# Handing a PEER kernel a second, transposed copy of its expert table

## The chip, the cores and the metric

The kernel runs on one core of one Trainium2 chip. The metric is the device time of one execution in microseconds (us). Three runs of the kernel before took 2838.91, 2841.39 and 2841.68 us; the median is 2841.39 us.

## The reference, cut to what matters

The reference is a decoder block over 1024 tokens of 1024 features (and 16 meta tokens ahead of them): a mixer of short convolutions, and behind it a layer of 16384 single-neuron experts. Only the second part is touched. For each token a router picks 8 x 16 experts by product keys (`e1 * 128 + e2`) with a gate for each; `u` and `v` are tables of 16384 rows of 1024.

```python
idx = e1 * PEER_N_KEYS + e2
gates = jax.nn.softmax(vals.astype(jnp.float32), axis=-1).astype(q.dtype)
...
u_sel = jnp.take(u, idx, axis=0)
act = jax.nn.gelu(jnp.einsum("chkd,cd->chk", u_sel, xc))
v_sel = jnp.take(v, idx, axis=0)
return jnp.einsum("chk,chkd->cd", act * gates, v_sel)
```

The result is added to the stream `h`, and a last RMS norm with the gain `final_norm_g` gives the output.

## The kernel before, in words

Tokens go in eight tiles of 128. The five tiles `ND` take the experts densely: every token against all 16384 experts, in 128 chunks of 128 experts (`NK` chunks), weighted with a gate matrix that is zero where the router chose nothing. The three tiles `NG` gather: for each token its 128 rows of `u` and then of `v` are fetched from DRAM, one indirect DMA of 128 rows at a time (L590, issued by POOL), and each fetched block is worked off by one VectorE instruction (L613 for `u`, L639 for `v`). Both ways run side by side.

There are three stages. `front` (mixer, router scores, up to about 700 us) is not touched but for where its constants lie. `gate_matrix` (L656, some 700 to 990 us) builds the gate matrix with TensorE products of one-hot tiles (L693 to L710) and writes it to DRAM; between its steps it lets the generator `hidden_ahead` (L762) run, which computes the `u` products of the 16 chunks in `AHEAD` and parks their gelu in DRAM. `dense` (L784, 990 us to the end) runs over the 128 chunks.

All matrix products are of three passes in 32-bit: each operand is split into a rounded part `hi` (a ScalarE copy, L156) and a rest `lo` (a subtraction, L157, on VectorE or on the engine given), and `mm3` (L183 to L190) multiplies hi by hi, hi by lo and lo by hi.

One chunk of `dense` that is not in `AHEAD` goes so. The chunk of `u` lies in DRAM as 128 experts x 1024 features, but the product needs features on the partitions. So `prep_u` (L729) loads it to `raw` (one pool tag of three buffers, which the chunks of `v` use too), transposes four 128x128 blocks on TensorE into a PSUM bank of the pool `ptr` (L735), and splits that bank to `uhi` and `ulo`; twice a chunk, `q` = 0 and 1, for the chunk that comes next. The product of all 640 dense tokens is made in two segments of 320 columns, each in a PSUM bank `mm` of the pool `pmm` (two banks). The order is q outside, segment inside: q0 of both segments, then q1 of both; each `hidden` call is 12 matmuls of 320 columns (four blocks, three passes), so 48 a chunk. When a segment is complete, ScalarE makes the gelu (L842), VectorE weighs it with the gates (L825), and it is split to `phi` and `plo`. Then the chunk of `v` is loaded and split to `vhi` and `vlo`. After each four chunks `down` (L801) makes the second product: 5 token tiles x 2 halves, each 12 matmuls of 512 columns into a bank `ms` (pool `pms`, four banks), added to `acc` by VectorE (L809).

Between these steps `advance(n)` moves the stream of the gather on by n blocks: three a chunk, one for an `AHEAD` chunk, and `PACE` says how many behind each piece of `down`. A block is fetched (eight buffers `g` in the pool `gb`) and used six blocks later. When a token tile is done, `finish` (L648) makes the last norm with `gfin`, a 128-fold copy of `final_norm_g` that is loaded once, and stores the rows. The dense tiles are finished one after the other in the last `down`.

`hidden_ahead` has its own preparation, `prep_ahead` (L740): four transposes (L747), a ScalarE copy to `uhi` (L751), one more TensorE product that subtracts `uhi` in the bank by way of the constant `minus` (L752), and a second ScalarE copy to `ulo` (L753). Its products go to banks of `pms`.

The order of each engine's instructions is laid down when the program is built, by a planner that follows the order of the code and its priorities; each engine, and each DMA queue, then takes its instructions in that order. The loads of `u`, `v` and the gates all go by SyncE's queue (SP).

## Time and profile before

| | before |
|---|---|
| median of three runs | 2841.39 us |
| the profiled execution's own time | 2840.61 us |
| its span in the profile | 2838.8 us |
| TensorE matmul (PE) busy, share of the span | 2700.6 us, 95% |
| VectorE (DVE) busy | 2443.3 us, 86% |
| ScalarE (ACT) busy | 897.6 us, 32% |
| GpSimd (POOL) busy | 913.7 us, 32% |
| bytes moved by DMA | 684.08 MB |
| of them the gather's indirect DMAs | 402.70 MB |

How to read it: busy time is a sum over the whole span, and the stages differ. Matmuls are pipelined, so one of them lasts longer in the profile than the time until the next one starts; where the text counts what a matmul costs, it takes the distance of starts. The page has 40 slices of equal length with the busy tenths of each engine; windows give the same for stretches that one chooses; groups of instructions carry the mean length of one and the idle time of the engine just before them.

### The profile page before, as it was taken

The page shows a single profiled execution, that of the slowest core. Times are in us where ns is not written, and L with a number is a line of the kernel's source. Part 1 is how long each engine was busy: PE and PEld are TensorE (multiplying, and loading weights), DVE is VectorE, ACT ScalarE, POOL GpSimd, SP SyncE. Part 2 cuts the span into 40 slices and gives each one's busy share as a digit, 9 for nine tenths or more (in the row PEclk, how much of TensorE's full clock was granted, in tenths as well). Part 3 has the DMA queues.
Part 4 walks back from the last instruction along what each step waited for, and adds up shares of the span by engine and source line. Part 5 has one row for each costly group of instructions (what it writes and reads, how often), then busy time and mean ns, then how long its engine had stood idle before and what let it go on. Part 6 is the DMA issues. An engine that isn't in the chain of part 4 may idle for free.

```text
span 2838.8 us, 43868 instructions
## 1 busy us (share of the span) xinstructions
PE 2700.6 (95%) x16513; PEld 2483.4 (87%) x16513; DVE 2443.3 (86%) x5152; ACT 897.6 (32%) x1764; POOL 913.7 (32%) x793
## 2 busy tenths in 40 slices
PE   6999999998999889999999999999999999999998
PEld 5999889987999878988888889888888888888887
DVE  5998667997988778899889889889998888989986
ACT  4112531115998622222222222222222222222222
POOL 0000011110000034455444544445545544545440
PEclk9999999998999999999999999999999999999999
DMA  3111321102576798999989999989999999989992
GB/s 114 45 45 61 103 104 39 38 16 79 156 199 196 229 343 310 335 324 327 331 307 333 313 326 336 331 304 355 329 332 315 331 328 322 324 300 331 327 326 77
DMA packets 299540, 684.08 MB, mean 241 GB/s; under 512 B 20617, under 2 KB 153737, under 8 KB 299328
## 3 DMA queue, kind: packets, MB, share of 16 engines
q0 software_dynamic: 110592, 402.70, 39.7%
q1 hardware_dynamic: 188256, 276.92, 29.2%
q8 instruction: 130, 2.13, 0.3%
q10 hardware_dynamic: 480, 1.65, 0.2%
q14 instruction: 82, 0.67, 0.1%
HBM read 624.05 MB, written 57.15 MB: 240 GB/s over the span
## 4 chain that ended last, share of the span: by engine, by line
PE 67%; DVE 16%; DMA 10%; ACT 4%; issue 2%; SPq 0%; DVEq 0%; ACTq 0%
PE ms L190 12%; PE ms L189 12%; PE ms L188 12%; DMA raw<-in_peer_v_dram 8%; PE mm L190 7%; PE mm L188 7%; PE mm L189 7%; PE mm L707 4%; DVE row L639 3%; DVE vlo L157 2%; PE tr L735 2%; DVE g L613 1%; DMA raw<-in_peer_u_dram 1%; DVE s L469 1%; ACT vhi L156 1%
## 5 line engine op out<-in xcount | busy, mean ns | idle before, releaser
L590 POOL DMA_INDIRECT g<-in_peer_u_dram,ix x384 | 433.5, 1129 | 801.1 <-DVE g L613 374.6
L188 PE MATMUL mm<-nhi,uhi 128*128 128x320 f32 x1792 | 572.4, 319 | 30.2 <-ACT p L842 30.1
L590 POOL DMA_INDIRECT g<-in_peer_v_dram,ix x384 | 438.2, 1141 | 457.2 <-DVE row L639 388.7
L190 PE MATMUL mm<-nhi,ulo 128*128 128x320 f32 x1792 | 557.7, 312 | 17.8 <-DVE ulo L157 17.0
L189 PE MATMUL mm<-nlo,uhi 128*128 128x320 f32 x1792 | 554.1, 309 | 0.0
L188 PE MATMUL ms<-vhi,phi 128*128 128x512 f32 x1280 | 501.1, 391 | 1.5 <-ACT phi L156 1.5
L190 PE MATMUL ms<-vhi,plo 128*128 128x512 f32 x1280 | 498.4, 390 | 0.0
L189 PE MATMUL ms<-vlo,phi 128*128 128x512 f32 x1280 | 498.4, 389 | 0.0
L639 DVE SCALAR_TENSOR_TENSOR row<-g,w,row 128x1024 f32<-128x1024 f32 x384 | 492.1, 1281 | 6.8 <-DMA row<-hd 5.5
L613 DVE SCALAR_TENSOR_TENSOR g<-g,row 128x1024 f32<-128x1024 f32 x384 | 464.5, 1222 | 0.0
L188 PEld LDWEIGHTS mm<-nhi,uhi 128*128 128x128 f32 x1792 | 337.9, 189 | 40.1 <-ACT p L842 38.4
L190 PEld LDWEIGHTS mm<-nhi,ulo 128*128 128x128 f32 x1792 | 337.1, 188 | 28.2 <-DVE ulo L157 28.0
L189 PEld LDWEIGHTS mm<-nlo,uhi 128*128 128x128 f32 x1792 | 338.2, 189 | 1.2
L156 ACT CAST phi<-p 128x320 fp32r<-128x320 f32 x256 | 116.3, 459 | 563.5 <-PE ms L189 340.9
L188 PEld LDWEIGHTS ms<-vhi,phi 128*128 128x128 f32 x1280 | 240.3, 188 | 51.0 <-ACT phi L156 2.4
L190 PEld LDWEIGHTS ms<-vhi,plo 128*128 128x128 f32 x1280 | 240.3, 188 | 50.7 <-DVE plo L157 0.5
L189 PEld LDWEIGHTS ms<-vlo,phi 128*128 128x128 f32 x1280 | 240.4, 188 | 49.1
L156 ACT CAST vhi<-raw 128x1024 fp32r<-128x1024 f32 x128 | 132.9, 1050 | 461.1 <-PE ms L190 316.2
L809 DVE TENSOR_TENSOR acc<-acc,ms 128x512 f32<-128x512 f32 x320 | 219.3, 685 | 34.8 <-PE ms L190 34.0
L157 POOL TENSOR_TENSOR wlo<-wraw,whi 128x1024 fp32r<-128x1024 f32 x16 | 38.0, 2377 | 570.5 <-ACT whi L156 570.5
L157 DVE TENSOR_TENSOR vlo<-raw,vhi 128x1024 fp32r<-128x1024 f32 x128 | 156.3, 1221 | 64.9 <-ACT vhi L156 64.8
L157 DVE TENSOR_TENSOR ulo<-tr,uhi 128x512 fp32r<-128x512 f32 x224 | 153.5, 687 | 43.5 <-ACT uhi L156 42.9
(208 smaller groups left out, 4943.6 us busy)
## 6 DMA issues: line engine op xcount, KB each, us to landing
raw<-in_peer_u_dram SPq DMA_DIRECT2D x128, 512.0 KB, 6.3
raw<-in_peer_v_dram SPq DMA_DIRECT2D x128, 512.0 KB, 6.5
gd<-st SPq DMA_DIRECT2D x40, 1024.0 KB, 9.1
g<-gd SPq DMA_DIRECT2D x64, 640.0 KB, 7.4
wraw<-in_w_in_dram SPq DMA_DIRECT2D x20, 512.0 KB, 4.3
wraw<-in_peer_w_q_dram SPq DMA_DIRECT2D x16, 512.0 KB, 4.1
g<-in_peer_u_dram,ix POOLq DMA_INDIRECT x384, 6.2
g<-in_peer_v_dram,ix POOLq DMA_INDIRECT x384, 6.2
```

The lines of the kernel that those rows point to most:

```text
L156: nc.scalar.copy(hi, src)
L157: self.mark(eng.tensor_tensor(lo, src, hi.bitcast(F32), op=OP.subtract))
L188: self.nc.tensor.matmul(ps, lh(a), rh(b), start=first and i == 0, stop=False)
L189: self.nc.tensor.matmul(ps, lh(a), rl(b), start=False, stop=False)
L190: last = self.nc.tensor.matmul(ps, ll(a), rh(b), start=False, stop=final and i == n - 1)
L469: nc.vector.match_replace(s2, v[:, 0:8], s, NEG)
L590: self.nc.gpsimd.indirect_dma_start(out=g, out_offset=None, in_=self.t[table][0], in_offset=bass.IndirectOffsetOnAxis(ap=ix, axis=0))
L613: self.after(nc.vector.scalar_tensor_tensor(ut, ut, 1.0, b["x"], op0=OP.mult, op1=OP.mult, accum_out=b["act"][:, k:k + 1]))
L639: self.after(nc.vector.scalar_tensor_tensor(b["h"], b.pop(k), res[0][:, k:k + 1], b["h"], op0=OP.mult, op1=OP.add))
L707: nc.tensor.matmul(pg[:, :, m], o2[:, 4 * z + m, :], o1[:, 4 * z + m, :], start=True, stop=True)
L735: self.nc.tensor.transpose(ps[:, k, :], self.raw[:, (4 * q + k) * P:(4 * q + k + 1) * P], self.ident)
L809: self.mark(V.tensor_tensor(acc[:, i, dd], acc[:, i, dd], po, op=OP.add))
```

## The change

`kernel()` makes a second layout of `u` on the host and hands it over as an input `peer_ut`: for each chunk 128 rows (features within a block) by 1024 (8 blocks of 128 experts), so that a chunk lands in SBUF as the product needs it. The gather reads `peer_u` as before.

- `prep_u` and `prep_ahead` go, with their transposes and the constant `minus`. `load_u` loads a chunk of `peer_ut` into a tag `uraw` of two buffers, and `split_u` splits it whole, 128x1024, from SBUF. `uhi` and `ulo` are 128x1024 with two buffers (before 128x512 with three). In `hidden_ahead` the rest `ulo` is made by GpSimd.
- `load_v` has the tag `raw` for itself, with two buffers.
- The order of a chunk's product is now segment outside, q inside. In `dense` the first segment has its bank in `pmm` and the second in `ptr`, so each has two; in `hidden_ahead` both are in `ptr`, two banks in place of the four of `pms`.
- A chunk's `u` is loaded two chunks ahead and split one chunk ahead, behind the first 12 of the 48 matmuls of the chunk before it.
- `advance` is called as often as before: three times a chunk.
- `gfin` goes. `finish` loads `final_norm_g` each time, by SyncE's queue into one of the eight buffers `g` of the gather.
- The constants are given up before the gather's pools are opened; `nT` is allocated ahead of them.

The diff, without the removed `load`, `prep_u` and `prep_ahead`:

```diff
@@ -64,7 +64,6 @@
         self.ctx, self.tc, self.nc, self.t = ctx, tc, tc.nc, t
         self.n = 0
         self.last = {}
-        self.const = ctx.enter_context(self.pool("const", 1))
         self.small = ctx.enter_context(self.pool("small", 2))
         self.keep = ctx.enter_context(self.pool("keep", 1))
         self.ptr = ctx.enter_context(self.pool("ptr", 2, space=PSUM))
@@ -94,8 +93,6 @@
         make_identity(nc, self.ident)
         self.identb = self.tile(const, [P, P], BF16, "identb")
         nc.scalar.copy(self.identb, self.ident)
-        self.minus = self.tile(const, [P, P], F32R, "minus")
-        nc.scalar.mul(self.minus, self.ident, -1.0)
         self.ones = self.tile(const, [P, P], F32, "ones")
         nc.vector.memset(self.ones, 1.0 / C)
         nrow = SCW + CFW + 5
@@ -581,10 +578,6 @@
             yield from self.gather_up(r, w)
             yield from self.gather_down(r, w)
 
-    def gather_constants(self):
-        self.gfin = self.tile(self.ga, [P, D], F32, "gfin", bufs=1)
-        self.nc.scalar.dma_start(self.gfin, self.t["final_norm_g"].rearrange("(o d) -> o d", o=1).broadcast_to([P, D]))
-
     def fetch(self, table, ix):
         g = self.tile(self.gb, [P, D], F32, "g")
         self.nc.gpsimd.indirect_dma_start(out=g, out_offset=None, in_=self.t[table][0],
@@ -647,7 +640,9 @@
 
     def finish(self, ti, h):
         o = self.tile(self.ga, [P, D], F32, "row")
-        self.row_norms([(o, h, P)], self.gfin, None)
+        g = self.tile(self.gb, [P, D], F32, "g")
+        self.nc.sync.dma_start(g, self.t["final_norm_g"].rearrange("(o d) -> o d", o=1).broadcast_to([P, D]))
+        self.row_norms([(o, h, P)], g, None)
         self.nc.sync.dma_start(self.t["out"][0, ti * P:(ti + 1) * P], o)
 
     def key_bank(self):
@@ -721,64 +716,50 @@
             for _ in ahead:
                 pass
 
...
+    def load_u(self, c):
+
+        r = self.tile(self.de, [P, D], F32, "uraw", bufs=2)
+        self.nc.sync.dma_start(r, self.t["peer_ut"][c * P:(c + 1) * P])
         return r
 
...
+    def load_v(self, c):
+        r = self.tile(self.de, [P, D], F32, "raw", bufs=2)
+        self.nc.sync.dma_start(r, self.t["peer_v"][0, c * NK:(c + 1) * NK])
+        return r
+
+    def split_u(self, raw, eng=None):
+        hi, lo = (self.tile(self.de, [P, D], F32R, "u" + s, bufs=2) for s in ("hi", "lo"))
+        self.split(hi, lo, raw, eng=eng)
         return hi, lo
 
     def hidden(self, ps, uT, q, s):
 
         (hi, lo), (xh, xl) = uT, self.nT
-        self.mm3(ps, (lambda a: hi[:, a, :], lambda a: lo[:, a, :]), (lambda b: xh[:, b, s], lambda b: xl[:, b, s]),
-                 [(k, 4 * q + k) for k in range(4)], q == 0, q == 1)
+        at = lambda u: lambda k: u[:, k * NK:(k + 1) * NK]
+        self.mm3(ps, (at(hi), at(lo)), (lambda k: xh[:, k, s], lambda k: xl[:, k, s]),
+                 [(k, k) for k in range(4 * q, 4 * q + 4)], q == 0, q == 1)
 
     def hidden_ahead(self, pool):
 
         T = ND * P
         segs = segments(T)
-        uT = self.prep_ahead(AHEAD[0], 0)
+        raws = [self.load_u(c) for c in AHEAD[:2]]
+        uT = self.split_u(raws.pop(0), eng=self.nc.gpsimd)
         for i, c in enumerate(AHEAD):
-            pu = [self.tile(self.pms, [P, 512], F32, "ms")[:, :s.stop - s.start] for s in segs]
-            for q in range(2):
-                cur = uT
-                for s, ps in zip(segs, pu):
+            pu = [self.tile(self.ptr, [P, 512], F32, "tr")[:, :s.stop - s.start] for s in segs]
+            cur = uT
+            for j, (s, ps) in enumerate(zip(segs, pu)):
+                for q in range(2):
                     self.hidden(ps, cur, q, s)
                     if q == 1:
                         p = self.tile(pool, [P, segs[0].stop], F32, "pa")[:, :s.stop - s.start]
                         self.nc.scalar.activation(p, ps, AF.Gelu_apprx_tanh)
                         self.nc.sync.dma_start(self.p_d[i, :, s], p)
-                    if s is segs[0]:
-                        if q == 0:
-                            uT = self.prep_ahead(c, 1)
-                        elif i + 1 < len(AHEAD):
-                            uT = self.prep_ahead(AHEAD[i + 1], 0)
+                    if j == 0 and q == 0:
+                        if raws:
+                            uT = self.split_u(raws.pop(0), eng=self.nc.gpsimd)
+                        if i + 2 < len(AHEAD):
+                            raws.append(self.load_u(AHEAD[i + 2]))
                     yield
 
     def dense(self, stream):
@@ -812,7 +793,8 @@
                         self.finish(i, acc[:, i, :])
 
             main = [c for c in range(NK) if c not in AHEAD]
-            uT = [self.prep_u(main[0], q) for q in range(2)]
+            raws = [self.load_u(c) for c in main[:2]]
+            nxt = self.split_u(raws.pop(0))
             for c in range(NK):
                 if c % 2 == 0:
                     gg = self.tile(de, [P, T // GB_T, 2, GB_T], F32, "g")
@@ -833,24 +815,28 @@
                     advance(AHD)
                 else:
                     main.pop(0)
-                    pu = [self.tile(self.pmm, [P, 512], F32, "mm")[:, :s.stop - s.start] for s in segs]
-                    for q in range(2):
-                        for s, ps in zip(segs, pu):
-                            self.hidden(ps, uT[q], q, s)
+                    uT = nxt
+                    for j, s in enumerate(segs):
+                        ps = self.tile(*((self.pmm, [P, 512], F32, "mm"), (self.ptr, [P, 512], F32, "tr"))[j % 2])
+                        ps = ps[:, :s.stop - s.start]
+                        for q in range(2):
+                            self.hidden(ps, uT, q, s)
                             if q == 1:
                                 p = self.tile(dn, [P, segs[0].stop], F32, "p")[:, :s.stop - s.start]
                                 nc.scalar.activation(p, ps, AF.Gelu_apprx_tanh)
                                 weigh(s, p)
+                            if j or q:
                                 advance(1)
-                        if main:
-                            uT[q] = self.prep_u(main[0], q)
-                        if q == 0:
-                            advance(1)
+                            if j == 0 and q == 0:
+                                if main:
+                                    nxt = self.split_u(raws.pop(0))
+                                if len(main) > 1:
+                                    raws.append(self.load_u(main[1]))
                 if len(pend) == GRP:
                     down()
                     pend = []
                 vh, vl = (self.tile(dn, [P, D], F32R, "v" + s, bufs=GRP) for s in ("hi", "lo"))
-                self.split(vh, vl, self.load("peer_v", c))
+                self.split(vh, vl, self.load_v(c))
                 pend.append((ph, pl, vh, vl))
             for _ in stream:
                 pass
@@ -860,8 +846,10 @@
 def body(tc, t):
     with ExitStack() as ctx:
         b = Block(ctx, tc, t)
+        b.nT = b.pair(ctx.enter_context(b.pool("nT", 1)), ND * P, "n")
+        const_ctx = b.pool("const", 1)
+        b.const = const_ctx.__enter__()
         b.constants()
-        b.nT = b.pair(ctx.enter_context(b.pool("nT", 1)), ND * P, "n")
         route_ctx = b.pool("route", 2)
         with b.pool("wst", 2, right=True) as b.wst:
             first, routes = b.front(route_ctx)
@@ -869,9 +857,9 @@
         b.gate_matrix(first, routes[:ND - 1])
         gather = [b.token_experts(r) for r in routes[ND - 1:]]
         route_ctx.__exit__(None, None, None)
+        const_ctx.__exit__(None, None, None)
         b.ga = ctx.enter_context(b.pool("ga", 2))
         b.gb = ctx.enter_context(b.pool("gb", GB))
-        b.gather_constants()
         b.last = {}
         b.dense(b.stream(gather))
 
@@ -888,6 +876,9 @@
         a = np.ascontiguousarray(inputs[name])
         arrays[f"in_{name}_dram"] = a
         t[name] = nc.dram_tensor(f"in_{name}_dram", a.shape, mybir.dt.from_np(a.dtype), kind="ExternalInput").ap()
+    ut = np.ascontiguousarray(inputs["peer_u"][0].reshape(NK, NK, KD, P).transpose(0, 3, 2, 1).reshape(NK * P, D))
+    arrays["in_peer_ut_dram"] = ut
+    t["peer_ut"] = nc.dram_tensor("in_peer_ut_dram", ut.shape, F32, kind="ExternalInput").ap()
     t["out"] = nc.dram_tensor("out_0_dram", (1, SEQ, D), F32, kind="ExternalOutput").ap()
     with tile.TileContext(nc) as tc:
         body(tc, t)
```

25 lines of the change are left out of this document (removed).

## The prediction

> **What bounds the kernel now.** I read the page's busy shares and slices first, to see where the stages lie.
>
> ```profile
> span 2838.8 us, 43868 instructions
> ...
> PE   6999999998999889999999999999999999999998
> ...
> DVE  5998667997988778899889889889998888989986
> ...
> GB/s 114 45 45 61 103 104 39 38 16 79 156 199 196 229 343 310 335 324 327 331 307 333 313 326 336 331 304 355 329 332 315 331 328 322 324 300 331 327 326 77
> ```
>
> A slice is 71 us. TensorE (PE) is at nine tenths in nearly all of them, VectorE (DVE) at eight or nine, and from the fifteenth slice on, where the dense stage begins, the DMA moves 300 to 355 GB/s. The change works in the gate stage (some 700 to 990 us) and the dense stage, so I asked for windows of these and of the tail.
>
> ```profile
> core 0: us, PE busy (x) PEld busy (x) DVE busy (x) ACT busy (x) POOL busy (x), PEclk, DMA share, GB/s
> 700.00:990.00 290.00, 277.54 (x2220) 263.89 (x2219) 251.68 (x587) 243.82 (x595) 2.08 (x2) 0.99 0.66 188
> 990.00:2790.00 1800.00, 1738.93 (x9864) 1569.45 (x9863) 1592.78 (x2334) 449.01 (x833) 869.62 (x767) 1.00 0.91 323
> ```
>
> In the dense window, 1800 us long, PE is busy 1739 us, VectorE 1593 us, and the DMA engines 0.91 of the time. That is the difficulty of this case: PE is the bound, but two others stand close behind it. Next I took the groups of the dense window, each with its mean and with the idle time just before it.
>
> ```profile
> L188 PE MATMUL mm<-nhi,uhi 128*128 128x320 f32 x1757 | 561.2, 320 | 30.2 <-ACT p L842 30.1
> L190 PE MATMUL mm<-nhi,ulo 128*128 128x320 f32 x1758 | 547.2, 312 | 17.8 <-DVE ulo L157 17.0
> L639 DVE SCALAR_TENSOR_TENSOR row<-g,w,row 128x1024 f32<-128x1024 f32 x384 | 492.1, 1281 | 6.8 <-DMA row<-hd 5.5
> L188 PE MATMUL ms<-vhi,phi 128*128 128x512 f32 x1240 | 485.5, 392 | 1.5 <-ACT phi L156 1.5
> L809 DVE TENSOR_TENSOR acc<-acc,ms 128x512 f32<-128x512 f32 x310 | 212.5, 685 | 30.5 <-PE ms L190 29.7
> L157 DVE TENSOR_TENSOR vlo<-raw,vhi 128x1024 fp32r<-128x1024 f32 x125 | 152.6, 1221 | 58.5 <-ACT vhi L156 58.5
> L157 DVE TENSOR_TENSOR ulo<-tr,uhi 128x512 fp32r<-128x512 f32 x219 | 150.1, 687 | 43.5 <-ACT uhi L156 42.9
> L735 PE MATMUL tr<-ident,raw 128*128 128x128 f32 x872 | 131.7, 274 | 11.6 <-DMA raw<-in_peer_u_dram 11.5
> L156 ACT CAST vhi<-raw 128x1024 fp32r<-128x1024 f32 x125 | 129.8, 1050 | 450.7 <-PE ms L190 316.2 <-DMA raw<-in_peer_v_dram 134.5
> L156 ACT CAST uhi<-tr 128x512 fp32r<-128x512 f32 x219 | 128.0, 584 | 189.1 <-PE tr L735 185.7 <-PE mm L189 3.3
> L157 DVE TENSOR_TENSOR plo<-p,phi 128x320 fp32r<-128x320 f32 x252 | 123.4, 490 | 35.1 <-ACT phi L156 34.6
> L825 DVE TENSOR_TENSOR p<-p,g 128x320 f32<-128x320 f32 x252 | 121.8, 489 | 31.1 <-ACT p L842 30.9
> ```
>
> A matmul's own length says too much, since the next one starts before it ends. Two pieces of the timeline give the distances: the start of a row is its first column.
>
> ```profile
> 1604.65 0.31 PE L190 MATMUL mm<-nhi,ulo 128*128 128x320 f32 x1
> ...
> 1604.80 0.60 PE L735 MATMUL tr<-ident,raw 128*128 128x128 f32 x4
> ...
> 1605.15 0.39 PE L188 MATMUL mm<-nhi,uhi 128*128 128x320 f32 x1
> ...
> 1605.38 0.31 PE L189 MATMUL mm<-nlo,uhi 128*128 128x320 f32 x1
> ...
> 1605.53 0.31 PE L190 MATMUL mm<-nhi,ulo 128*128 128x320 f32 x1
> ...
> 2826.36 0.39 PE L188 MATMUL ms<-vhi,phi 128*128 128x512 f32 x1
> ...
> 2829.08 0.39 PE L188 MATMUL ms<-vhi,phi 128*128 128x512 f32 x1
> ```
>
> From 1605.38 to 1605.53 is one matmul of 320 columns: 0.147 us as the mean of many such steps, of which this row shows 0.15. From 1604.65 to 1605.53 there are three such steps and four transposes, 0.88 us; three steps alone are 0.44, so **a group of four transposes costs PE 0.44 us**. From 2826.36 to 2829.08 are 12 matmuls of 512 columns, 0.227 us each. In the window that makes 3 x 1757 x 0.147 = 775 us for the `u` products, 3 x 1240 x 0.227 = 844 us for `down`, and 872/4 = 218 groups x 0.44 = 96 us of transposes: 1715 of 1800 us. The other 85 us are PE waiting; the idle columns name 61 of them: 30.2 for a PSUM bank that ScalarE has not read yet, 17.8 for `ulo`, 11.6 for a load of `u`, 1.5 in `down`.
>
> **The change part by part. Transposes.** All 218 groups go: -96 us of PE in the dense window. They stand between the matmuls on PE's own queue, so none of it is hidden while PE is the bound. That the code without them still issues them can be excluded; the question is only what is late next.
>
> **PSUM banks and order.** A segment's bank was needed again one chunk on; each segment now has two banks, so a gelu may be a whole chunk late (48 x 0.147 = 7.1 us) before PE feels it. The 30.2 us go. The `ulo` of the next chunk was started at the middle of a chunk for its first half and at the end for its second; now the whole stands behind the first 12 matmuls, and 36 x 0.147 = 5.3 us of PE work cover it. Against that stand a ScalarE copy (1.05, from the `vhi` row, which has the same form), a subtraction (1.22, `vlo`), and one gather block ahead of it (1.28): 3.5 us. The 17.8 us I halve; the 11.6 us for the load move from PE to ScalarE's copy, where the loads now run two chunks ahead, and I count them as gone. PE alone would need 1800 - 96 - 30 - 9 - 12 = 1653 us.
>
> **VectorE.** 219 subtractions of 128x512 (150.1 us) become 109 of 128x1024 x 1.221 = 133 us, so its work is 1592.8 - 150.1 + 133.1 = 1576 us. It now idles 207 us, and the idle columns above name nearly all: `vlo` 58.5, `ulo` 43.5, `plo` 35.1, `p` 31.1, `acc` 30.5, `row` 6.8, together 205.5. What of that stays is the term on which the sum rests, and no row of before shows it. Below it is bounded by PE's 1653 us (77 us of idle), above by all of it staying (1576 + 207 = 1783 us). I take 10 of 43.5 for `ulo`, since its copy waits for no transpose any more; 40 of 58.5 for `vlo`, since `v` gets two buffers of its own but its split still waits for `down` to give up the four `v` buffers (the 316.2 us on ScalarE); 78 of the 96.7 of `plo`, `p` and `acc`, which are steps to ScalarE and PE and back that the change leaves, though PE will be earlier; 7 for `row`. That is 135, and **1711 us for the dense window, -89**. It is nearer to PE's end than to the other because `ulo` and `acc` wait for an engine that gets faster.
>
> **ScalarE** swaps 219 x 0.584 = 128 us for 109 x 1.05 = 114 us and is busy a quarter of the window; its in-order queue matters, not its load. On **SP's queue** the loads are the same in number and size (128 and 128 of 512 KB), `u` without its tie to the `v` buffers.
>
> **The gate stage** (groups of 640 to 990 us; the last is from the page):
>
> ```profile
> L693 DVE TENSOR_TENSOR o<-iota,ms 128x1024 f32<-128x1024 f32 x80 | 97.1, 1219 | 11.5 <-PE mm L707 10.1
> L702 DVE TENSOR_SCALAR o<-iota,eT 128x128 f32<-128x128 f32 x320 | 87.6, 343 | 0.0
> L695 DVE TENSOR_TENSOR ob<-iob,e1b 128x512 bf16<-128x512 bf16 x80 | 31.4, 421 | 0.7 <-ACT o L700 0.6
> L747 PE MATMUL tr<-ident,raw 128*128 128x128 f32 x128 | 22.1, 282 | 4.1 <-DMA raw<-in_peer_u_dram 3.9 <-ACT ulo L753 0.2
> L753 ACT CAST ulo<-tr 128x512 fp32r<-128x512 f32 x32 | 20.0, 632 | 3.6 <-PE tr L752 3.3
> L751 ACT CAST uhi<-tr 128x512 fp32r<-128x512 f32 x32 | 18.7, 586 | 28.5 <-PE tr L747 17.0 <-PE ms L189 11.3
> L752 PE MATMUL tr<-uhi,minus 128*128 128x512 f32 x32 | 15.5, 485 | 0.6 <-ACT uhi L751 0.5
> ...
> L157 POOL TENSOR_TENSOR wlo<-wraw,whi 128x1024 fp32r<-128x1024 f32 x16 | 38.0, 2377 | 570.5 <-ACT whi L156 570.5
> ```
>
> PE loses 32 groups of transposes (0.44) and 32 subtracting matmuls of 512 columns (0.227 by the distances, 0.485 by their length; I take 0.35): 25 us. ScalarE loses 38.7 us and gets 16 x 1.05 = 16.8. Four of the 16 chunks run before 700 us, where the router's VectorE work sets the pace, so three quarters count: -19 on PE, -16 on ScalarE, and VectorE has 252 of 290 us of its own. PE, ScalarE and VectorE take turns at being late here, so I take half, **-10**, with -19 and 0 as ends (the upper one below). GpSimd gets 16 x 2.377 = 38 us; its fetches begin at 990 us, and nothing queued behind these subtractions is due before.
>
> **The last norm.** Each of eight `finish` now loads 512 KB by SP into one of the eight gather buffers; on VectorE, L149 waits for it, and behind L149 the gather's blocks are queued.
>
> ```profile
> 2825.97 1.06 ACT L146 ACTIVATE row<-acc 128x1024 f32<-128x1024 f32 x1 [3.87 <-DVE acc L809]
> ...
> 2829.03 1.28 DVE L149 SCALAR_TENSOR_TENSOR row<-acc,rs,gfin 128x1024 f32<-128x1024 f32 x1
> ...
> gffn<-in_norm_ffn_g_dram ACTq DMA_DIRECT2D x1, 512.0 KB, 3.7
> ...
> raw<-in_peer_v_dram SPq DMA_DIRECT2D x128, 512.0 KB, 6.5
> ```
>
> The norm's own chain gives 3.1 us of cover (2825.97 to 2829.03). The same kind of load took 3.7 us, loads in the dense stage 6.5 us: 0.6 to 3.4 us too long if it is issued no earlier than the norm. Three finishes lie in the stream and of the last five only one can be felt, so 0 (issued early) to 14 us; I take **+3**.
>
> **Sum:** -89 - 10 + 3 = -96 on the profiled execution's 2840.6 us (its span 2838.8 and 1.8 around it), 2745 us. That execution lies 0.8 below the median of 2841.4, so the same serves for both.
>
> **The rivals.** *PE stays alone in front* (0.13): VectorE's waits shrink with its lag, the dense window falls to 1653 and the gate stage by 19: 2840.6 - 147 - 19 = 2675 us. For it: the gather's blocks (L639) waited for almost nothing. Against it: 77 us of idle would be 4.7% of a window in which VectorE has 11.5% now.
>
> *The DMA becomes the bound* (0.14). No byte goes: 323 GB/s x 1800 us = 581 MB must still pass. Of the slices of the dense stage only three pass 335 GB/s; held there, 581 MB take 1735 us, -65, so 2840.6 - 65 - 10 + 3 = 2769 us. Against it: one slice held 355.
>
> *The gate stage gives nothing* (0.08), because GpSimd's subtractions and VectorE's compares get in each other's way. In before the GpSimd subtraction ran in the router's stage only, so no row has it beside L695 or L702. If each of the twelve in the stage stops VectorE for its whole 2.377 us, VectorE has 252 + 28.5 = 280 us, and the 290 stay: 2755 us. The Trainium skill has such a rule on the page "SBUF — State Buffer", section "Who interferes with whom": a VectorE instruction with two inputs in SBUF and a GpSimd instruction that reads SBUF exclude each other, and the later waits for the whole of the other. By that rule this rival's 2755 would be the forecast; by the rows alone it is 2745, and no run here shows which.
>
> *Nothing is gained* (0.04): 0.91 of the DMA engines' time may be all that this mix of queues yields, and the gate stage may give nothing as well; then 2841 us.
>
> *Slower* (0.05): the place is ScalarE's queue. The copy to `uhi` now waits there for a load, and the gelus stand behind it. `vhi` shows what that looks like: 134.5 us of waiting for loads. Of the 5.3 us of cover above 1.7 are left over. If the planner issues the `u` loads so late that each copy waits half a load, 3.25 us, then 109 x 1.55 = 169 us come in, against -96 - 30 - 10 of gains: 2874 us. It decides from 1.7 + 136/109 = 2.9 us of mean wait. Against it stand two buffers and an issue two chunks ahead.
>
> **How the numbers follow.** The forecast's case has 0.56, by itself 2715 to 2775 (the idle of VectorE, 105 to 165, and -19 to 0 in the gate stage). 2695 to 2800 takes in the rivals on the DMA and the gate stage and a third of the first; outside remain 0.09 there, and 0.09 above. About 0.2% (5.7 us) is what a measurement of this kernel can tell from no change; the three runs lie within 0.1%. Faster 0.91, same 0.04, slower 0.05.
>
> **What would show it.** Right: no group with `ident` and a chunk of `u` behind 640 us; idle before L188 `mm` on the PSUM bank near 0; VectorE's idle in the dense stage near 135 us and its share 92%; GB/s near 340; the gate stage about 10 us shorter. Wrong: PE's idle grows to over 100 us with `ulo` or `uhi` behind it; gather blocks that wait for their fetch (then it is the DMA); L695 or L702 longer beside GpSimd.

## The result and the profile after

The kernel after takes 2756.91 us (median of four runs, 2748.82 to 2761.42), the kernel before 2841.53 us (four runs, 2838.91 to 2844.88). The ratio is 0.9698, its 95% interval 0.9672 to 0.9725: 85 us less, where 96 were forecast. The profiled execution of after took 2759.32 us. First its page, with the same rows that were shown of before:

```profile
span 2757.6 us, 41701 instructions
...
PE   6999989995999989999999999999999999999998
...
DVE  5998677999799979899999998989989989989996
...
GB/s 117 46 47 62 85 130 31 39 39 46 126 201 185 201 354 351 341 323 354 339 331 336 346 337 349 325 340 340 337 323 352 329 352 343 349 320 327 351 331 135
```

The shape is the old one: PE at nine tenths, VectorE close behind, the DMA a little faster than it was. The windows of the gate stage and of the dense stage:

```profile
core 0: us, PE busy (x) PEld busy (x) DVE busy (x) ACT busy (x) POOL busy (x), PEclk, DMA share, GB/s
700.00:990.00 290.00, 275.52 (x2175) 264.51 (x2175) 256.06 (x571) 223.21 (x539) 35.25 (x16) 0.98 0.66 191
990.00:2700.00 1710.00, 1638.39 (x8915) 1482.11 (x8914) 1563.75 (x2209) 429.36 (x718) 967.40 (x764) 0.98 0.93 340
```

By its marks in the trace the gate stage's last one-hot product ends at 971.3 us (968.1 before) and the last matmul of `down` starts at 2748.8 (2830.2 before). So the gate stage gave nothing (+3), the dense stage between these marks went from 1862.1 to 1777.5 us (-85), and what follows the last `down` stayed (8.6 us before, 8.8 after). The +3 itself is too small to read: runs shown below whose gate stage is the same code as after's end it between 965.3 and 972.7 us. VectorE idles 1710 - 1563.75 = 146 us in this window (135 forecast), the DMA moves 340 GB/s. The new column is PEclk: 0.98, where before had 1.00.

The groups of that window, from 990 to 2700 us, with the mean of one and the idle time ahead of the group:

```profile
L187 PE MATMUL mm<-nhi,ulo 128*128 128x320 f32 x879 | 284.1, 323 | 51.9 <-DVE ulo L154 51.9
L185 PE MATMUL mm<-nhi,uhi 128*128 128x320 f32 x879 | 282.2, 321 | 16.5 <-ACT uhi L153 11.6 <-DVE ix L548 4.9
...
L185 PE MATMUL tr<-nhi,uhi 128*128 128x320 f32 x864 | 267.0, 309 | 0.0
...
L790 DVE TENSOR_TENSOR acc<-acc,ms 128x512 f32<-128x512 f32 x307 | 209.0, 682 | 9.8 <-PE ms L187 8.7 <-PE ms L186 0.5
...
L154 DVE TENSOR_TENSOR vlo<-raw,vhi 128x1024 fp32r<-128x1024 f32 x124 | 150.9, 1219 | 65.3 <-ACT vhi L153 65.3
L154 DVE TENSOR_TENSOR ulo<-uraw,uhi 128x1024 fp32r<-128x1024 f32 x109 | 132.9, 1219 | 4.2 <-ACT uhi L153 4.0
L153 ACT CAST vhi<-raw 128x1024 fp32r<-128x1024 f32 x124 | 128.2, 1050 | 544.0 <-PE ms L187 304.4 <-DMA raw<-in_peer_v_dram 204.4 <-issue 22.0
...
L153 ACT CAST uhi<-uraw 128x1024 fp32r<-128x1024 f32 x110 | 115.2, 1047 | 77.5 <-PE tr L186 66.3 <-DMA uraw<-in_peer_ut_dram 8.8 <-issue 2.2
```

No group with `ident` is left, and PE's matmuls wait for a gelu (L826) no more. In the place of that stands a wait for `ulo` of 51.9 us (17.8 before) and one for `uhi` of 11.6. And ScalarE's copies of `v` wait 204.4 us for their loads, where they waited 134.5.

**One such stop close up.** A `down` ends at 1211.2 us. ScalarE's queue in the timeline behind it (start, length; in brackets what it waited for):

```profile
1209.39 2.01 ACT L153 CAST vhi<-raw 128x1024 fp32r<-128x1024 f32 x2 [18.82 <-PE ms L187]
1214.96 0.44 ACT L826 ACTIVATE p<-mm 128x320 f32<-128x320 f32 x1 [3.56 <-PE mm L187]
1221.71 1.05 ACT L153 CAST vhi<-raw 128x1024 fp32r<-128x1024 f32 x1 [6.31 <-DMA raw<-in_peer_v_dram]
1222.66 0.46 ACT L153 CAST phi<-p 128x320 fp32r<-128x320 f32 x1
1224.09 1.06 ACT L153 CAST vhi<-raw 128x1024 fp32r<-128x1024 f32 x1 [0.97 <-DMA raw<-in_peer_v_dram]
1225.04 0.43 ACT L826 ACTIVATE p<-tr 128x320 f32<-128x320 f32 x1
1225.37 1.04 ACT L153 CAST uhi<-uraw 128x1024 fp32r<-128x1024 f32 x1
```

While `down` reads the four `vhi`/`vlo` pairs, nothing of `v` can be split, and the two buffers of raw `v` stay full. Near its end two copies run one behind the other (1209.39), and only when the subtractions behind them give the raw buffers back do the next two loads start: SP's queue issues the first at 1214.21, and its copy begins 7.5 us later. In ScalarE's order their copies stand ahead of the second gelu and of `uhi`, so ScalarE stands still for 6.31 us, and `uhi` of the next chunk begins at 1225.37, when PE has already run out of work. VectorE's queue stops with it, since the subtraction to `vlo` stands there in the same place:

```profile
1222.79 1.23 DVE L154 TENSOR_TENSOR vlo<-raw,vhi 128x1024 fp32r<-128x1024 f32 x1 [5.33 <-ACT vhi L153]
...
1227.03 1.22 DVE L154 TENSOR_TENSOR ulo<-uraw,uhi 128x1024 fp32r<-128x1024 f32 x1
```

PE's side of it, in four windows:

```profile
core 0: us, PE busy (x) PEld busy (x) DVE busy (x) ACT busy (x) POOL busy (x), PEclk, DMA share, GB/s
1215.00:1225.00 10.00, 10.00 (x70) 10.00 (x69) 4.67 (x7) 2.72 (x4) 1.77 (x2) 1.00 0.79 277
1225.20:1228.20 3.00, 0.84 (x4) 0.32 (x3) 3.00 (x7) 2.01 (x4) 2.06 (x2) 0.97 0.52 168
1228.20:1231.20 3.00, 2.90 (x11) 2.90 (x12) 3.00 (x6) 0.97 (x2) 1.81 (x2) 0.50 0.87 317
1231.50:1236.00 4.50, 4.50 (x33) 4.50 (x32) 4.50 (x9) 1.28 (x4) 2.55 (x2) 1.00 1.01 381
```

PE works without a break, then four matmuls in 3 us, then 3 us at a granted clock of 0.50, then as before. In the half-clock stretch matmuls of 320 columns start 0.267 us apart instead of 0.147. By the starts of all matmuls in the trace (distances that are 0.2 us or more over the usual one), PE's stops between 1010 us and the last 60 us add up to 73 us in after; 26 places have over 1 us, up to 6.1, and 15 of them are followed by such a dip. In before they add up to 65 us, but in smaller pieces: 23 places have over 1 us, one of them 2.7, the others at most 2.2, and there is a single dip behind them. A dip lasts about 3.4 us (one lasts 6.8); at half clock 3.4 us cost PE some 1.5 us.

Is this stop like the others? In the 20 us ahead of each of the 26, ScalarE's queue stood still at a copy to `vhi` for 3.3 to 7.5 us, waiting for its load. In one point the stop shown is rare: of the 21 waits for `ulo` over 1 us, 19 found `uhi` copied 2.2 us or more before VectorE began `ulo`, and VectorE mostly busy in between. So the late thing was mostly VectorE's queue, which ScalarE's stop had held up, at `vlo` as here or at `p` and `plo`.

### The profile page after: what moved, and what is told of

The parts are those of the page before. It is cut to its first block, busy times and chain, and to the rows that moved or that the text cites. A ratio compares the mean times of both kernels' runs of the same rounds, so it can differ in the third digit from the quotient of the medians.

```text
span 2757.6 us, 41701 instructions
## 1 busy us (share of the span) xinstructions
PE 2593.0 (94%) x15457; PEld 2391.7 (87%) x15457; DVE 2444.6 (89%) x5040; ACT 857.4 (31%) x1597; POOL 1054.3 (38%) x809
## 4 chain that ended last, share of the span: by engine, by line
PE 51%; DVE 31%; DMA 9%; issue 6%; ACT 3%; SPq 0%; DVEq 0%; ACTq 0%
PE ms L187 8%; PE ms L186 8%; PE ms L185 8%; DVE g L606 8%; DMA raw<-in_peer_v_dram 7%; PE mm L702 4%; DVE row L632 4%; PE mm L187 4%; PE mm L185 4%; PE mm L186 4%; PE tr L187 3%; PE tr L186 3%; PE tr L185 3%; DVE vlo L154 2%; DVE acc L790 2%
## 5 line engine op out<-in xcount | busy, mean ns | idle before, releaser
L583 POOL DMA_INDIRECT g<-in_peer_u_dram,ix x384 | 499.2, 1300 | 402.6 <-DVE g L606 245.8
L583 POOL DMA_INDIRECT g<-in_peer_v_dram,ix x384 | 474.5, 1236 | 382.8 <-DVE row L632 331.4
L185 PE MATMUL tr<-nhi,uhi 128*128 128x320 f32 x1152 | 362.6, 315 | 14.7 <-ACT pa L756 13.5
L187 PE MATMUL tr<-nhi,ulo 128*128 128x320 f32 x1152 | 361.8, 314 | 1.3 <-POOL ulo L154 1.3
L186 PE MATMUL tr<-nlo,uhi 128*128 128x320 f32 x1152 | 362.5, 315 | 0.0
L187 PE MATMUL mm<-nhi,ulo 128*128 128x320 f32 x896 | 289.4, 323 | 51.9 <-DVE ulo L154 51.9
L185 PE MATMUL mm<-nhi,uhi 128*128 128x320 f32 x896 | 287.5, 321 | 16.5 <-ACT uhi L153 11.6
L186 PE MATMUL mm<-nlo,uhi 128*128 128x320 f32 x896 | 285.7, 319 | 0.0
L185 PEld LDWEIGHTS tr<-nhi,uhi 128*128 128x128 f32 x1152 | 219.2, 190 | 15.3 <-ACT pa L756 13.8
L187 PEld LDWEIGHTS mm<-nhi,ulo 128*128 128x128 f32 x896 | 176.8, 197 | 59.8 <-DVE ulo L154 59.1
```

The lines of the kernel that those rows point to most:

```text
L185: self.nc.tensor.matmul(ps, lh(a), rh(b), start=first and i == 0, stop=False)
L186: self.nc.tensor.matmul(ps, lh(a), rl(b), start=False, stop=False)
L187: last = self.nc.tensor.matmul(ps, ll(a), rh(b), start=False, stop=final and i == n - 1)
L583: self.nc.gpsimd.indirect_dma_start(out=g, out_offset=None, in_=self.t[table][0], in_offset=bass.IndirectOffsetOnAxis(ap=ix, axis=0))
```

## The experiments

Two theories of where the dense stage's rest went. **ScalarE's row:** copies of `v` that wait for loads stand ahead of the gelus and of `uhi`, so after each `down` PE stops, and its clock falls. **VectorE's pace** (the prediction's view): VectorE, with its work and some 135 us of idle that it cannot avoid, sets the stage; a wait that is taken from PE comes back as another. All ratios are to the kernel before on the same chip, with 95% intervals; a difference between two kernels is that of their medians, unless said. The medians of before on the chips used differ by 3 us (2840.9 to 2843.9), so for small differences the ratios are given too.

**One bank pair again** (e_bank). Both segments share `pmm`, as they did before:

```diff
-   ps = self.tile(*((self.pmm, [P, 512], F32, "mm"), (self.ptr, [P, 512], F32, "tr"))[j % 2])
+   ps = self.tile(self.pmm, [P, 512], F32, "mm")
```

> The changed kernel with one thing undone: both segments of a chunk's product take their banks from the one pool of two banks again, so that a bank is needed again one segment pair later. Theory A (the prediction's: the second pair of banks was worth the 30.2 us that the matmuls waited for the gelu): these waits come back, 20 to 40 us before the first pass of the u product with the gelu as releaser, and the time rises from 2757 to 2775 to 2795 us. Theory B (VectorE is the bound of the dense stage now, and a wait of TensorE for a bank only takes the place of its wait for ulo): the gelu waits come back but the ulo waits of 51.9 us shrink by as much, and the time stays within 6 us of 2757.

2764.74 us, ratio 0.9725 [0.9700, 0.9749], 8 us more than after, with intervals that overlap. Its groups from 990 to 2700 us:

```profile
L185 PE MATMUL mm<-nhi,uhi 128*128 128x320 f32 x1753 | 554.1, 316 | 58.0 <-ACT p L826 55.4 <-DVE ix L548 2.2
...
L187 PE MATMUL mm<-nhi,ulo 128*128 128x320 f32 x1754 | 548.6, 314 | 11.2 <-DVE ulo L154 11.0
```

The wait for a gelu is back with 55.4 us, and the wait for `ulo` has shrunk to 11.0. The two waits stand in for each other: as the VectorE theory said, but the row theory too can have both come from one late queue, ScalarE's. This run alone doesn't tell them apart.

**The gate stage's subtractions on VectorE** (e_lo_dve), at both places:

```diff
-   uT = self.split_u(raws.pop(0), eng=self.nc.gpsimd)
+   uT = self.split_u(raws.pop(0), eng=self.nc.vector)
```

> The changed kernel with one thing undone: in the gate stage the rest ulo of the 16 chunks worked ahead is made by VectorE in place of GpSimd. Theory A (GpSimd's subtraction and VectorE's instructions with two inputs in SBUF, or the scalar compares, stop each other): the compares of 128x128 that took 1487 ns beside a GpSimd subtraction and 339 ns else are all at about 340 ns, and the 4.2 us multiplications of the one-hot tiles at 2.28; VectorE gets 16 x 1.22 = 19.5 us more of its own and is rid of about 25 us of being stopped; the gate stage ends 0 to 10 us earlier and the time is 2747 to 2757 us. Theory B (the long compares have another cause, as a late operand from ScalarE or TensorE): they stay long, VectorE carries 19.5 us more in a stage where it is at nine tenths, and the time is 2765 to 2780 us.

2744.23 us, ratio 0.9653 [0.9634, 0.9673], 12.7 us less than after, better than expected; the gate stage's mark comes at 952.4 us, 19 earlier. Groups from 640 to 990 us, first of after:

```profile
L697 DVE TENSOR_SCALAR o<-iota,eT 128x128 f32<-128x128 f32 x320 | 102.3, 386 | 0.0
...
L523 DVE TENSOR_TENSOR oh<-oh,lst 128x4096 bf16<-128x4096 bf16 x8 | 22.3, 2783 | 0.1
```

and of this run:

```profile
L697 DVE TENSOR_SCALAR o<-iota,eT 128x128 f32<-128x128 f32 x320 | 87.4, 340 | 0.0
...
L154 DVE TENSOR_TENSOR ulo<-uraw,uhi 128x1024 fp32r<-128x1024 f32 x19 | 23.2, 1219 | 7.6 <-ACT uhi L153 7.5
...
L523 DVE TENSOR_TENSOR oh<-oh,lst 128x4096 bf16<-128x4096 bf16 x8 | 18.3, 2284 | 0.0
```

Those means hide a few long ones. In after's timeline one of each kind stands out:

```profile
658.75 2.53 POOL L154 TENSOR_TENSOR ulo<-uraw,uhi 128x1024 fp32r<-128x1024 f32 x1 [5.46 <-ACT uhi L153]
...
659.14 4.29 DVE L523 TENSOR_TENSOR oh<-oh,lst 128x4096 bf16<-128x4096 bf16 x1
...
695.13 4.31 DVE L697 TENSOR_SCALAR o<-iota,eT 128x128 f32<-128x128 f32 x8
...
695.45 2.37 POOL L154 TENSOR_TENSOR ulo<-uraw,uhi 128x1024 fp32r<-128x1024 f32 x1 [32.83 <-ACT uhi L153]
```

L523 takes 2.28 us when it is alone and 4.29 beside GpSimd's subtraction; eight compares that take 2.14 us elsewhere in the stage take 4.31, 2.2 more, about the length of the subtraction (2.37). In five places a compare of L697 that started within 0.14 us of a subtraction's start took 2.40 to 2.51 us instead of 0.34, to about the subtraction's end. VectorE's instructions add up to 376 us in this window in after, and to 373 - 23 = 350 in this run without its own subtractions: it had lost some 25 us to GpSimd's sixteen, while doing them itself takes 16 x 1.22 = 20 us. VectorE's compare with an input in PSUM (L688) kept its 1.22 us. So the prediction's rival on the gate stage held. The Trainium skill says on the page "SBUF — State Buffer", section "Who interferes with whom", that a VectorE instruction with two inputs in SBUF contends with a GpSimd instruction that reads SBUF, one with at most one (outside the modes with two ports) does not, and who comes first has the shared ports for its whole instruction. The trace agrees for L523 and L688; which case the compares of L697 are, it does not show.

The 19 us are more than was gained. In after the sixth `oh` of L523 runs at 942.0 us, ahead of the mark; in this run it runs at 955.1, behind it. So a piece of the router's work changed sides. PE's first product of the dense stage starts at 982.0 us against 989.2, and its first `down` at 1011.1 against 1024.8, 14 earlier, which is near the 12.7 of the time. VectorE's own balance, 25 lost against 20 of work, is about 5 us of that; where the rest comes from stays open.

**Another order on ScalarE** (e_v_order). The load of `v` stays where it was; the split is put off into the next chunk, where it stands behind that chunk's `uhi` copy by a dependency that orders and does not wait. `split_v` is called behind `split_u`, at the start of a chunk of `AHEAD`, and before the last `down`:

```diff
+   def split_v():
+       if late:
+           ph, pl, raw = late.pop()
+           vh, vl = (self.tile(dn, [P, D], F32R, "v" + s, bufs=GRP) for s in ("hi", "lo"))
+           self.split(vh, vl, raw, behind=self.ucopy)
+           pend.append((ph, pl, vh, vl))
...
-   self.split(vh, vl, self.load_v(c))
-   pend.append((ph, pl, vh, vl))
+   late.append((ph, pl, self.load_v(c)))
```

> The changed kernel with another order on ScalarE: the copy to vhi of a chunk is put behind the copy to uhi that the next chunk issues, so that no row of vhi copies stands ahead of a uhi copy after down; no work is added or left out. Theory A (behind each down, ScalarE's queue stands still at vhi copies whose loads of v could start only when down gave up the v buffers, and the next chunk's uhi, hence ulo, comes late; TensorE's clock is halved for 3.4 us after such a stop): TensorE's waits for ulo and uhi, together 64 us, fall under 25 us, the dips of the clock in the dense stage from 14 to under 5, and the time to 2695 to 2725 us. Theory B (VectorE is the bound of the dense stage whatever the order): the waits go to other places, its idle stays near 130 us, and the time stays between 2745 and 2765 us. Theory C (the DMA is the bound): the loads land later, gather blocks wait for their fetch, and the time stays over 2740 us.

2670.15 us, ratio 0.9385 [0.9370, 0.9401]: 87 us less than after (89 by the ratios), with the same work, the same loads and the same buffers; more than the row theory expected. Its groups from 990 to 2600 us:

```profile
L190 PE MATMUL mm<-nhi,ulo 128*128 128x320 f32 x865 | 269.1, 311 | 2.6 <-DVE ulo L157 2.6
L188 PE MATMUL mm<-nhi,uhi 128*128 128x320 f32 x864 | 269.0, 311 | 7.2 <-ACT uhi L153 7.2
...
L157 DVE TENSOR_TENSOR vlo<-raw,vhi 128x1024 fp32r<-128x1024 f32 x124 | 151.0, 1218 | 1.1 <-ACT vhi L153 1.1
...
L153 ACT CAST vhi<-raw 128x1024 fp32r<-128x1024 f32 x123 | 127.8, 1047 | 501.3 <-PE ms L190 469.7 <-DMA raw<-in_peer_v_dram 31.7
```

The waits for `ulo` and `uhi` fall from 51.9 and 11.6 to 2.6 and 7.2 us, `v`'s wait for its loads from 204.4 to 31.7, VectorE's wait for `vhi` from 65.3 to 1.1. Two clock dips are left of 15, and some 7 us of stops of 73. These 66 us and 13 dips of some 1.5 us make 86; between its marks the dense stage became 83.6 us shorter (1693.9 against 1777.5). The window of its dense stage:

```profile
990.00:2610.00 1620.00, 1605.53 (x8871) 1456.06 (x8870) 1559.48 (x2206) 433.29 (x713) 989.24 (x760) 0.99 0.96 357
```

VectorE does the same 1560 us of work in 1620 us: it is busy for 96%, with 60 us of idle. That cannot be if 135 us of idle were unavoidable, so VectorE's pace falls as the cause in after. The edit does two things, the later place in the code and the dependency; they were not run apart. And it moves the subtraction to `vlo` on VectorE's queue along with the copy on ScalarE's: what is shown is that the place of `v`'s split is the cause, not how much of it each of the two queues did by itself.

**A third buffer for raw `v`** (e_raw3g7), paid for with one gather buffer:

```diff
-GB, LAG = 8, 6
+GB, LAG = 7, 5
...
-   r = self.tile(self.de, [P, D], F32, "raw", bufs=2)
+   r = self.tile(pool, [P, D], F32, "raw", bufs=3)
```

> The changed kernel with three buffers in place of two for the chunks of v as loaded; to make room the gather has seven buffers in place of eight and a block is used five blocks after its fetch. Theory A (the late loads of v after each down are the cause of TensorE's waits for ulo): one more chunk of v is in place when down ends, the wait of ScalarE for loads of v falls from 204 to under 130 us, TensorE's waits for ulo from 52 to under 35 us, and the time to 2725 to 2750 us. Theory B (VectorE is the bound): 2750 to 2765 us. Theory C (the DMA is the bound): the smaller number of fetches in flight makes it worse, over 2765 us, with gather blocks that wait for their fetch.

2748.53 us, ratio 0.9658 [0.9642, 0.9675], 8 us less than after. In the view of waits, from 990 to 2640 us:

```profile
ACT vhi L153 <- DMA raw<-in_peer_v_dram: 156.7, 30, 9.8
...
PE mm L187 <- DVE ulo L154: 41.1, 27, 4.2
```

In after the same window has 196.6 and 49.5. The time is inside the range expected, but the waits fell less than was said (156.7 against under 130, 41.1 against under 35). A load that starts earlier, at the price of a gather buffer, helps a little; the change of the copy's place helped eight to ten times as much.

**Order, and the subtractions on VectorE** (e_best): both edits above.

> The order of e_v_order and the subtraction on VectorE of e_lo_dve together. The two act in different stages, so their gains should add: 2670.2 less the 12.7 us between 2756.9 and 2744.2 is 2657 us; 2650 to 2664. If in the dense stage something else is now the bound whatever comes before it, a stage that starts 10 us earlier still ends 10 us earlier, so less than 6 us of gain would say that the 12.7 us were not the gate stage's.

2663.34 us, ratio 0.9370 [0.9348, 0.9393], the lowest time of this study, though its interval overlaps with e_v_order's: 6.8 us less by the medians, 4 by the ratios, where 12.7 were added up. The expectation took under 6 us as a sign that the 12.7 were not the gate stage's; between 4 and 7 that is not decided. The gate stage's mark comes 12.5 us earlier than in e_v_order (952.8 against 965.3), but here too a piece of the router's work went behind it: the first `down` starts 7.0 us earlier (1014.7 against 1021.7), and the last one 3 (2656.2 against 2659.1). Where these 4 us went in the dense stage stays open.

**What bounds the kernel once the order is mended?** Three runs on top of e_v_order. In e_order_half_u every second chunk of `u` is not loaded, its products taking the chunk before:

```diff
-   r = self.tile(self.de, [P, D], F32, "uraw", bufs=2)
-   self.nc.sync.dma_start(r, self.t["peer_ut"][c * P:(c + 1) * P])
+   n, r = getattr(self, "held", (0, None))
+   if n == 0:
+       r = self.tile(self.de, [P, D], F32, "uraw", bufs=2)
+       self.nc.sync.dma_start(r, self.t["peer_ut"][c * P:(c + 1) * P])
+   self.held = (1 - n, r)
```

> The order of e_v_order, and every second chunk of u is not loaded: its products are made from the chunk before it, so the output is not the reference's. That takes 64 x 0.524 = 34 MB of the dense and gate stages' transfers away (29 MB in the dense stage, 5% of its some 580), and no work of an engine. Theory A (TensorE and VectorE set the time, the transfers have room): 2670 within 8 us. Theory C (at a DMA share of 0.96 and 358 GB/s the transfers set it): up to 5% of the 1640 us of the dense stage, so 2590 to 2645 us.

2663.49 us, ratio 0.9369 [0.9346, 0.9392]: 6.7 us less, 5 by the ratios, whose intervals overlap. In e_order_nog VectorE does not weigh the second segment of a chunk with its gates:

```diff
-   V.tensor_tensor(pv, pv, g[:, s.start // GB_T:s.stop // GB_T], op=OP.mult)
+   if s.start == 0:
+       V.tensor_tensor(pv, pv, g[:, s.start // GB_T:s.stop // GB_T], op=OP.mult)
```

> The order of e_v_order, and the second segment of each chunk is not weighed with its gates: 128 multiplications of 128x320 on VectorE are left out, and the output is not the reference's. At the 0.41 us from one to the next that is 52 us less for VectorE, and no transfer and no TensorE work less. Theory A (TensorE sets the time in the dense stage, VectorE at 96% still has room): 2670 within 8 us. Theory B (VectorE sets it): 2625 to 2650 us.

2664.47 us, ratio 0.9377 [0.9353, 0.9400]: 5.7 us less, 2 by the ratios, whose intervals overlap. The dense window of e_order_half_u:

```profile
990.00:2610.00 1620.00, 1607.63 (x8874) 1458.40 (x8873) 1561.31 (x2207) 430.80 (x711) 998.98 (x760) 1.00 0.93 340
```

and that of e_order_nog:

```profile
990.00:2610.00 1620.00, 1606.71 (x8907) 1460.09 (x8906) 1524.35 (x2088) 429.29 (x720) 1010.52 (x761) 1.00 0.96 359
```

17 GB/s less from the DMA, or 35 us less work on VectorE, each bring no more than 7 us: neither sets the pace. The test from the other side adds work to PE: eight products per chunk whose result nothing reads, in after (e_trans) and in e_v_order (e_order_trans):

```diff
+   if q == 0:
+       tr = self.tile(self.pms, [P, 512], F32, "ms")
+       for k in range(4):
+           blk = uT[0][:, (4 * j + k) * P:(4 * j + k + 1) * P].bitcast(F32)
+           nc.tensor.matmul(tr[:, k * P:(k + 1) * P], blk, blk, start=True, stop=True)
```

> The changed kernel with TensorE work put back that nobody reads: in each chunk of the dense stage two groups of four products of 128x128 into a bank of pms, of the length and number of the transposes that the change took away (224 groups, 0.44 us each, 98 us). Theory A (TensorE sets the time except in the 64 us in which it waits for ulo and uhi behind down, and there the longer chunk gives the copies more time): 2757 and 50 to 98 us more, 2807 to 2855. Theory B (VectorE or the DMA set the time and TensorE has room): less than 50 us more.

2879.76 us, ratio 1.0126 [1.0099, 1.0153]: 123 us more than after, above what either theory expected. The reason is in the group from 990 to 2800 us, with the `ulo` wait above it:

```profile
L187 PE MATMUL mm<-nhi,ulo 128*128 128x320 f32 x874 | 274.6, 314 | 16.5 <-DVE ulo L154 16.4
...
L834 PE MATMUL ms<-uhi 128*128 128x128 f32 x1728 | 230.2, 277 | 0.0
```

The kernel writes 896 such products, and the whole trace has 1792 records of them (1728 in this window): in plain f32 each product is two instructions, 0.111 us apart by their starts. A group of four costs 8 x 0.111 = 0.89 us, not the 0.44 that four transposes cost, and 224 groups put 199 us on PE instead of the 98 meant. So of 199 us that were added 123 are felt; 76 went into what PE waited anyway, and the `ulo` wait shows it, 51.9 to 16.5.

> The order of e_v_order, with the TensorE work that nobody reads put back (224 groups of four products of 128x128 in the dense stage, 98 us). Theory A (TensorE sets the time of the dense stage there): 2670 and 80 to 100 us more, 2750 to 2770. Theory B or C (VectorE or the DMA set it): TensorE has its waits of some 23 us and whatever room the others leave, and the time rises by less than 50 us.

2853.8 us (eight runs), ratio 1.0048 [1.0034, 1.0062]; by the ratios 0.0663 x 2842 = 188 us more than e_v_order, of 199 that were added; both theories had counted on 98. With the order mended PE's work is felt almost whole: PE sets the dense stage.

**The old layout with the new order** (e_before_order): the same `split_v` in the kernel before.

> The kernel before, transposes and all, with the order of e_v_order on ScalarE: the copy to vhi of a chunk is put behind the copy to uhi that the next chunk issues. Theory A (the row of vhi copies behind down, waiting for loads, was there before too and made part of the 85 us of waits of TensorE in the dense stage): its idle before the first pass of the u products and before ulo falls from 48 to under 20 us, and the time from 2842 to 2785 to 2815 us; the new layout by itself is then worth the rest down to 2670, 115 to 145 us. Rival (the row only hurts where u is split whole from SBUF and its copy stands behind the vhi copies): 2842 within 8 us.

2832.8 us (ten runs), ratio 0.9967 [0.9954, 0.9980]: 9 us less than before, where the row theory expected 27 to 57 and its rival at most 8. Its groups from 990 to 2790 us:

```profile
L191 PE MATMUL mm<-nhi,uhi 128*128 128x320 f32 x1781 | 570.3, 320 | 0.0
...
L738 PE MATMUL tr<-ident,raw 128*128 128x128 f32 x880 | 134.5, 276 | 54.2 <-DMA raw<-in_peer_u_dram 53.6
```

The wait for a gelu and its bank, 30.2 us in before, is gone without a second bank pair. That alone shows little: PE now waits 53.6 us for loads of `u` (11.5 before), since in that kernel `u` and `v` share three raw buffers and `v` now holds its own longer. So e_before_sep takes that away: two buffers for `u`, two for `v`, and the room for them from `finish`, which loads its gain as after does.

```diff
-   r = self.tile(self.de, [P, D], F32, "raw", bufs=3)
+   r = self.tile(self.de, [P, D], F32, "raw" if table == "peer_v" else "uraw", bufs=2)
```

> The kernel before, transposes and all, with everything of e_v_order but the new layout's own parts: the order on ScalarE, two buffers for u as loaded and two for v in place of three for both, and the gain of the last norm loaded at each finish. Theory A (the 62.6 us that TensorE waited for loads of u in e_before_order come of the three shared buffers; with them gone the old layout runs nearly without waits, and what is left to e_v_order are the transposes at 0.44 us for a group of four): TensorE's waits in the dense stage fall from 73 to under 30 us and the time to 2765 to 2795 us, so the layout by itself is worth 95 to 125 us. Theory B (loads of u wait for something else, as their place in the queue behind loads of v): over 2815 us.

2765.26 us, ratio 0.9733 [0.9713, 0.9754], at the lower end of the range expected. From 990 to 2720 us:

```profile
L191 PE MATMUL mm<-nhi,uhi 128*128 128x320 f32 x1764 | 562.2, 319 | 0.0
L193 PE MATMUL mm<-nhi,ulo 128*128 128x320 f32 x1765 | 546.5, 310 | 1.8 <-DVE ulo L160 1.8
...
L740 PE MATMUL tr<-ident,uraw 128*128 128x128 f32 x876 | 131.7, 273 | 7.8 <-DMA uraw<-in_peer_u_dram 7.8
```

With one bank pair no wait for a gelu is left in L191, and no other wait has taken its place. The old layout, transposes and all, comes within 10 us of after (8.4 by the medians, 10 by the ratios), once its queue is in order and its buffers are apart. Between this run and e_v_order only the layout and what goes with it differ: 99 us by the ratios, 95 by the medians and between the marks of the dense stage (1789.3 against 1693.9).

**One bank pair with the order mended** (e_order_bank): e_bank's edit on e_v_order.

> The order of e_v_order with both segments' banks from the one pool of two, as in e_bank. Theory A (the row of vhi copies was what made a gelu late, by it or by a wait for ulo; with the row gone a bank is free in time in either way): 2670 within 8 us, and TensorE waits under 15 us for the gelu. Theory B (the second pair of banks is worth its 30 us once the waits for ulo no longer cover it): 2690 to 2710 us.

2676.08 us, ratio 0.9424 [0.9402, 0.9446]; 11 us more than e_v_order by the ratios, 6 by the medians. From 990 to 2600 us:

```profile
L188 PE MATMUL mm<-nhi,uhi 128*128 128x320 f32 x1757 | 544.3, 310 | 4.3 <-ACT p L840 4.1
```

With one bank pair PE waits 4.1 us for gelus, where e_bank had 55.4. The gelus were late because of the row, and a second bank pair mostly bore with that; 6 to 11 us of its own are left to it.

## Why the prediction was right, and where it was wrong

The time fell inside the range and its sign was the likeliest, but three of its steps failed (the halved wait for `ulo`, the reason for VectorE's idle time, the gate stage), and the dense stage came out near its sum for another reason than it gave.

- **Transposes, -96: right.** 95 to 99 us lie between e_before_sep and e_v_order, where little else differs.
- **"The 30.2 us go": gone, but worth little.** The wait for the bank went; in its place came that for `ulo`. Putting one bank pair back costs 8 us, within overlapping intervals, and 6 to 11 once the order is mended.
- **"The 17.8 us I halve": failed.** PE waited 51.9 us for `ulo` and 11.6 for `uhi`. The cover of 5.3 us against 3.5 was worked out for a ScalarE and a VectorE that are free when `uhi` and `ulo` are due, but for one gather block (1.28). They aren't: the `v` copies wait up to 7.5 us for loads that start only when `down` gives buffers up, VectorE stops at what hangs on them, and in the dense stage `ulo` begins 2.96 us (median) after `uhi` ends. The prediction saw `v`'s 134.5 us of such waits and used them as a picture of what loads of `u` could do, not as what stands ahead of `uhi`. Its slower rival had the place, ScalarE's queue, and the wrong load: `uhi` waited 8.8 us for its own.
- **VectorE's idle, 135: the size was near (146), the reason failed.** The parts were 65.3 for `vlo` (40 forecast), 4.2 for `ulo` (10), 69.1 for `plo`, `p` and `acc` (78; 40.9, 18.4 and 9.8 measured), 8.1 for `row` (7). But much of this idle was what ScalarE's row made, not what VectorE needs: e_v_order has 60 us. That -85 came so close to -89 is therefore luck. By the counts that the program writes, 5376 products of 320 columns and 3840 of 512 take 790 + 872 = 1662 us at the distances of the prediction; before spends 1862 - 1662 - 99 of transposes = 101 us beside that, after 1777 - 1662 = 115, e_v_order 1694 - 1662 = 32 (17 to 19 us of each pass behind the mark, in the last 96 products with `identb`). So after gives back 14 of the 99 us in stops and half clock, and leaves the hundred of before where it was.
- **PE alone in front, 2675: not in after, but it is what the order was worth.** e_v_order reaches 2670.
- **The gate stage, -10: failed.** The rival held: the stage ended 3 us later, within the spread of its code, and the sign that the prediction named for it came: the compares of L697 (L702 before) went from 87.6 to 102.3 us. Taking the subtractions back to VectorE brought the kernel 12.7 us, near what the prediction had counted for the stage (-10, with -19 as its bound).
- **The last norm, +3: about 0.** L146, which has L149's place, waited 0.1 us in the dense window, and the stretch behind the last `down` grew by 0.1 to 0.2.
- **The DMA as the bound: no.** 340 GB/s in after, 357 in e_v_order, and fewer bytes there bring no more than 7 us.

What stays open: what made up the rest of e_lo_dve's gain, why 7 us at the first `down` of e_best reach the end as 3, and how much ScalarE's queue and VectorE's each did; and the kernel before with buffers of its own for `u` and `v`, but the old order, was not run.

## What to carry to other kernels

When work is taken from the bound engine, look at what stands ahead of the next copy that it needs, on each in-order queue: behind an event that frees several buffers at once, copies that wait for loads may stand ahead of the copy that is urgent, and no column of busy time shows that. An order can be tested alone, with a dependency and no change of work; here that was worth 87 us, as much as the whole change to the layout. A queue that stops hands its stop on: here PE mostly waited for VectorE, which had waited for ScalarE, which had waited for a load. A wait that vanishes from one row and comes up in another (bank, then `ulo`) points to one cause behind both.

## What the runs showed of the hardware

- **The clock falls after short stops.** 0.84 us of PE work in 3 us, in two stops of 1.14 and 1.44 us, was followed by about 3.4 us at a granted clock of 0.50. The other 14 dips of after follow single stops of 2.0 to 6.1 us, while six stops of 2.4 to 3.3 us were followed by none. So in these two traces the same waiting cost more in longer pieces: 73 us of stops brought 15 dips in after, 65 us in smaller pieces one in before. The Trainium skill, page "TensorE: Matmul & The Clock Gate", section "What's actually happening", gives a window of about 3.4 us in which activity is watched, which is the length of the dips; and says that it runs freely, which fits that some stops bring a dip and others of the same length none. Its table names one idle window as the condition; here PE worked for a quarter of the 3 us ahead of the dip.
- **VectorE can stand still for the whole of a GpSimd subtraction**, also at a compare of one small f32 tile: 2.40 to 2.51 us instead of 0.34 in five places, beside subtractions of 2.36 to 2.47; a compare with an input in PSUM kept its 1.22 us.
- **A plain f32 product of 128x128 is two matmul instructions** 0.111 us apart, 0.89 us for four products, where four transposes of f32 cost 0.44.
